# Other constants in the estimate that resumes background work in a hybrid decoder layer (one core of Trainium2)

## The chip, the core and the metric

The program runs on one core of one Trainium2 chip. A core has a matrix engine (TensorE, PE in the profile), a vector engine (VectorE, DVE), a scalar engine (ScalarE, ACT), GpSimd (POOL) and a queue engine (SyncE, SP) from which most of the DMA transfers are issued. Each engine works through its own instructions in order. The metric is the device time of one execution in microseconds.

## The reference

One step of one decoder layer, for a new sequence of 512 tokens ("prompt") and for eight sequences that each get one new token ("sample"), with the same weights, in float32:

```python
mod = silu(c) @ w_ada + b_ada                      # 6 x 2048 modulation values per sequence
h = modulate(rmsnorm(x, g_norm_mix), sh1, sc1)
proj = h @ w_in                                    # 2048 -> 1536 + 3360 columns
att = banded_attention(q, k, v, sinks)             # 16 heads, window 128, ALiBi
rw, S, last_row = rwkv7_mix(p_rwkv, ...)           # 16 heads, S_t = S diag(w) + (S a) b^T + v k^T
x = x + gt1 * (concat(att, rw) @ w_out)
h2 = modulate(rmsnorm(x, g_norm_ffn), sh2, sc2)
gate, up = split(h2 @ w_ffn_in)
x = x + gt2 * ((silu(gate) * up) @ w_ffn_out)      # 5632 hidden
y = rmsnorm(x, g_norm_final)
```

The outputs are y, the last keys and values, the RWKV states and the last projection rows, for prompt and sample.

## The kernel before

**Main work.** All 520 columns (512 prompt tokens and 8 sample tokens) are kept as two halves of 260. Each weight tile of 128 output columns is worked off in slices of 128 rows of the contraction. `unit` loads four slices of weights (256 KB), copies them to a rounded high part (`wh`, on ACT) and the remainder (`wl`, on DVE), and `mm3` issues six matmuls of 260 columns for one slice: high weights with the high and the low part of the activations, low weights with the high part, each for two halves. This text calls these six a *slice* of main work. `main_tile` runs 16 slices for a tile of `w_in` or `w_ffn_in`; `part_tile`, `wout_part` and `wout_half` do the same for pieces of `w_in` during the start-up and for `w_out`.

**Background work.** Everything else before the FFN is written as Python generators that run while the program is built: the modulation weights (`h_part` with `ada_part` in the start-up, `ada_gen` for the other four sixths), the preparation of RWKV for one pair of heads (`rwkv_prep1`, `rwkv_prep2`), the triangular solve and then the chain over 16 chunks of 32 tokens (`rwkv_rest`), the RWKV of the samples, the attention of prompt and sample, the loading of the concatenated result and half of the second norm. A generator issues some instructions, then yields.

**The estimate.** After each slice the kernel calls `pump`. It adds the assumed time of a slice to an estimated TensorE clock (`now`) and resumes, in the order of their start, each generator whose last instructions should be done by then (`job[1] <= now`). Background instructions go through `Paced` objects (`self.px`): each call of an engine adds an assumed duration, a base and a part per column, to that engine's estimated clock, not before the instruction before it in the same step is done (`spent`), and 0.1 for the way to the next engine. So a step's instructions are reckoned one after the other. For the modulation weights, whose matmuls don't go through `Paced`, the durations are written out. The estimate exists only while the program is built: it decides the order in which instructions are issued, and leaves no instruction in the program. A later pass of the compiler puts them in the order in which each engine runs them, and moves instructions that it thinks not ready behind others.

**The stages.** Up to about 151 us (start-up), the first modulation values and the first five tiles of `w_in` are made in five stages of 2, 2, 4, 4 and 4 slices per tile, with the modulation of the next stage behind each (`h_part`, and `drain` at its end). Then 22 tiles of `w_in` are made in the order that RWKV needs, with RWKV pairs, solve, chain and `ada_gen` behind them; 12 more tiles (`spills`, queries, keys and values) are put in where RWKV is late and otherwise at the end. One chain step (two per chunk) is two small matmuls with a tile position, a DVE and an ACT instruction that move the result to `Z`. One step of `ada_gen` is a DMA of 256 KB and four matmuls with a tile position; it yields twice after each. From about 925 us, `wout_part` runs with the attention behind it, and `wout_half` with half of the norm. The FFN, from about 1240 us, has its order written out and calls no `pump`.

Of the kernel before, what the change touches and what calls it, by code (L numbers as in the profile page):

```python
# [8 lines left out]
F32R = mybir.dt.float32r  # L9
# [22 lines left out]
class Paced:  # L32


    def __init__(self, kern, eng, per, base):
        self.kern, self.eng, self.per, self.base = kern, eng, per, base

    def __getattr__(self, name):
        f = getattr(self.eng, name)

        def call(out, *a, **kw):
            if name == "dma_start":
                self.kern.spent(self.eng, 1.0, 1.5)
            else:
                per = self.per
                if name == "matmul" and a[0].dtype == F32R:
                    per /= 4
                self.kern.spent(self.eng, self.base + per * math.prod(out.shape[1:]), 0.1)
            return f(out, *a, **kw)  # L49
        return call  # L50


class PacedCore:
    def __init__(self, kern):
        nc = kern.nc
        self.nc = nc
        self.tensor = Paced(kern, nc.tensor, 0.0017, 0.06)
        self.vector = Paced(kern, nc.vector, 0.0011, 0.08)
        self.scalar = Paced(kern, nc.scalar, 0.001, 0.2)
        self.gpsimd = Paced(kern, nc.gpsimd, 0.0023, 0.1)  # L60
        self.sync = Paced(kern, nc.sync, 0, 0)


class Kern:
    def __init__(self, tc, I, O, upto="all"):
        self.tc, self.nc, self.I, self.O, self.upto = tc, tc.nc, I, O, upto
        self.n = 0
        self.bg = []
        self.free, self.done_at = {}, 0.0
        self.px = PacedCore(self)  # L70
        self.nada = 0
        self.sample_done = self.kv_done = self.decode_done = False
        self.cat_out, self.cat_in = set(), 0
        self.psc = None
        self.squares = [None, None]
# [44 lines left out]
        self.free[self.nc.tensor] = self.free.get(self.nc.tensor, 0.0) + us  # L120
        return self.free[self.nc.tensor]

    def pump(self, us=0.62):

        self.now(us)
        for job in list(self.bg):
            if job[1] > self.now():
                continue
            self.done_at = self.now()
            if next(job[0], "end") == "end":  # L130
                self.bg.remove(job)
            job[1] = self.done_at

    def start(self, gen):
        self.bg.append([gen, 0.0])
# [136 lines left out]
    def ada_part(self, f):  # L272

        nc = self.nc
        ps = self.aux_c(f // 2 % 2)
        for kg in range(4):
            tag, n = (("RR", 2), ("L3", 3), ("As", 1), ("L3", 3), ("RR", 2), ("L3", 3))[self.nada % 6]
            self.nada += 1
            raw = self.rc.tile([P, 1024], F32, tag=tag, bufs=n, name=self.nm("araw"))
            nc.sync.dma_start(raw, self.I["w_ada1"][f // 2, kg])  # L280
            self.ada_mm(ps, raw, kg, 0, 256)
            self.spent(nc.tensor, 0.45)
            self.done_at += 0.7
            yield
        yield from self.ada_finish(f, 2, ps)
# [9 lines left out]
    def ada_gen(self):  # L295
        nc = self.px
        for c in (GT1, SH2, SC2, GT2):
            for q in range(4):
                ci = c // 4 + q
                ps = self.hold("ada")  # L300
                for k in range(KD):
                    raw = self.w.tile([P, 512], F32, tag="ar", bufs=3, name=self.nm("ar"))
                    nc.sync.dma_start(raw, self.I["w_ada2"][ci - 8, k])
                    for j in range(4):
                        self.nc.tensor.matmul(
                            ps[32 * j:32 * j + 32, 0:128], self.cT[:, k, :], raw[:, j * 128:(j + 1) * 128],
                            start=k == 0, stop=k == KD - 1, tile_position=(0, 32 * j), skip_group_check=True,
                        )
                    self.spent(self.nc.tensor, 0.3)
                    yield  # L310
                    yield
                res = self.w.tile([P, 512], F32, tag="ar", bufs=3, name=self.nm("adar"))[:, 0:128]
                nc.scalar.copy(res, ps[:, 0:128])
                yield
                p2 = self.aux("adT")
                nc.tensor.transpose(p2[:, 0:128], res, self.ident)
                nc.vector.tensor_tensor(
                    self.mod[:, 4 * ci:4 * ci + 4, :], p2[:, 0:128].rearrange("p (f t) -> p f t", f=4)[:, :, 0:9],
                    self.par[:, P_BA + 4 * ci:P_BA + 4 * ci + 4].unsqueeze(2).broadcast_to([P, 4, 9]), ALU.add)
# [963 lines left out]
    def wout_half(self, h, kept):  # L1283

        while self.cat_in < KD:
            self.pump()
        for o in range(0, KD, 2):
            mt = lambda: self.ps_m.tile([P, 2, 512], F32, tag="m", name=self.nm("po"))
            ps = mt()
            for j in range(2):  # L1290
                if o + j not in kept:
                    pool = dict(pool=self.wk, bufs=6) if o in (2, 6, 10) else {}
                    u = self.unit(self.I["w_out"][o + j, :, 12 * 128:16 * 128], **pool)
                    if pool:
                        kept[o + j] = u
                wh, wl = kept.get(o + j, u)
                for kk in range(4):
                    s = slice(kk * 128, (kk + 1) * 128)
                    self.mm3(ps, P, wh[:, s], wl[:, s], *self.cat[1], kk, kk == 0, kk == 3, ((h, j),))
                    self.pump(0.4)  # L1300
                if o == KD - 2:
                    self.accumulate_half(o + j, 1, ps[:, j:j + 1], GT1, h)
                    ps = mt()
            if o < KD - 2:
                self.accumulate_half(o, 2, ps, GT1, h)
# [233 lines left out]
```

## Time and profile before

| | us |
|---|---|
| median of 3 runs | 2763.02 |
| lowest, highest | 2754.31, 2765.76 |
| the profiled execution | 2761.62 |
| its span, first to last instruction | 2759.8 |

The rows of the profile used here have these forms. A row of the order of time gives start, duration (us), engine, line, operation, what is written from what, shapes, and how many instructions are merged; a bracket gives the idle time ahead and what ended it. A float32 matmul that isn't in the rounded format has two records each, so `psc<-Z,L x4` is one chain step of two matmuls (the first step of a chunk; `psc<-Z,LS` is the second), and `ada<-ar,cT x8` is one ada group of four. `pm` are main matmuls. A row by stretch gives the stretch and its length, then the busy time of PE, of the weight loads (PEld), DVE, ACT and POOL with their instructions, the granted TensorE clock (1.00 is full speed), the share of the DMA engines' time, and GB/s. A row of waits gives the waiting engine, tile and line, what it waited for, the total, how often, and the longest. Durations of matmuls overlap, so distances are taken from start to start. A few matmul records can be missing.

### The profile page before, as it was taken

Reading aid. Unit: us, or ns where it says so; the run is one execution under the profiler, and the core shown is the slowest. Engines: PE = TensorE matmul, PEld = TensorE weight load, DVE = VectorE, ACT = ScalarE, POOL = GpSimd, SP = SyncE. Lnnn points to the kernel's source line nnn. Section 1 sums busy time; section 2 is a strip of 40 time slices with the busy share of each in tenths; the row PEclk is TensorE's granted clock in tenths of the full one; section 3 lists DMA queues with packets and bytes.
Section 4 is the critical chain, followed back from the end, with each engine's and each line's share of the span. In section 5 each row is a group of like instructions: output and inputs, shape, how many; then the busy total and the mean of one; then the engine's idle time right before and its main releaser. Section 6 shows DMA issues by size and latency. Waiting matters only on the chain.

```text
span 2759.8 us, 58911 instructions
## 1 busy us (share of the span) xinstructions
PE 2679.3 (97%) x24461; PEld 2479.0 (90%) x24461; DVE 1356.5 (49%) x3266; ACT 923.4 (33%) x1816; POOL 223.6 (8%) x300
## 2 busy tenths in 40 slices
PE   7899999999999999989999999999999999999998
PEld 5577777887787898979999999999999999999997
DVE  2465677767755465682434343434343434343436
ACT  3133445455432344552222222222222222222225
POOL 1012122222111000130000000000000000000004
PEclk9899999999989999999999999999999999999999
DMA  8865554555556732322222222222222222222223
GB/s 296 308 200 149 153 152 141 161 150 151 175 163 206 255 133 100 113 80 92 91 93 90 93 92 93 92 92 93 92 93 92 92 93 92 93 92 93 90 96 110
DMA packets 189900, 354.25 MB, mean 128 GB/s; under 512 B 27665, under 2 KB 38849, under 8 KB 189345
## 3 DMA queue, kind: packets, MB, share of 16 engines
q1 hardware_dynamic: 185584, 339.30, 37.1%
q0 software_dynamic: 3408, 10.15, 1.2%
q8 instruction: 191, 3.13, 0.5%
q10 hardware_dynamic: 640, 1.05, 0.1%
q14 instruction: 77, 0.62, 0.1%
HBM read 332.86 MB, written 18.55 MB: 127 GB/s over the span
## 4 chain that ended last, share of the span: by engine, by line
PE 59%; DVE 2%; DMA 1%; ACT 1%; POOL 0%; issue 0%; DVEq 0%; SPq 0%; ACTq 0%; POOLq 0%
PE pm L98 36%; PE pf L98 18%; PE po L98 3%; PE pl L49 1%; PE pO L49 0%; PE pt L49 0%; PE psc L49 0%; DVE wl L91 0%; DVE x L1178 0%; DMA raw<-in_w_fi 0%; DVE h2L L49 0%; DVE u L49 0%; ACT h2H L49 0%; DMA raw<-in_w_out 0%; POOL u L49 0%
## 5 line engine op out<-in xcount | busy, mean ns | idle before, releaser
L88 ACT CAST wh<-raw 128x512 fp32r<-128x512 f32 (+2 forms) x751 | 460.9, 615 | 1266.8 <-PE pm L98 807.1
L91 DVE TENSOR_TENSOR wl<-raw,wh 128x512 fp32r<-128x512 f32 (+2 forms) x751 | 522.3, 697 | 690.2 <-ACT wh L88 688.8
L98 PE MATMUL pm<-h2H,wh 128*128 128x260 f32 x2816 | 571.2, 282 | 2.2 <-ACT wh L88 1.2
L98 PE MATMUL pm<-h2L,wh 128*128 128x260 f32 x2816 | 572.1, 283 | 0.7 <-DVE h2L L49 0.4
L98 PE MATMUL pm<-h2H,wl 128*128 128x260 f32 x2816 | 572.4, 283 | 0.0
L98 PEld LDWEIGHTS pm<-h2H,wh 128*128 128x128 f32 x2816 | 435.9, 188 | 2.9 <-ACT wh L88 1.3
L98 PEld LDWEIGHTS pm<-h2L,wh 128*128 128x128 f32 x2816 | 435.0, 188 | 1.7 <-DVE h2L L49 1.5
L98 PEld LDWEIGHTS pm<-h2H,wl 128*128 128x128 f32 x2816 | 436.3, 188 | 0.0
L98 PE MATMUL pm<-hH,wh 128*128 128x260 f32 (+1 forms) x1248 | 297.6, 318 | 2.8 <-ACT hH L143 1.6
L98 PE MATMUL pf<-gH,wh 128*128 128x260 f32 x1312 | 266.8, 283 | 0.0
L98 PE MATMUL pf<-gH,wl 128*128 128x260 f32 x1312 | 266.4, 282 | 0.0
L98 PE MATMUL pf<-gL,wh 128*128 128x260 f32 x1312 | 266.4, 282 | 0.0
L98 PE MATMUL pm<-hL,wh 128*128 128x260 f32 (+1 forms) x1248 | 264.7, 292 | 0.2 <-DVE hL L144 0.2
L98 PE MATMUL pm<-hH,wl 128*128 128x260 f32 (+1 forms) x1248 | 262.5, 291 | 0.0
L98 PEld LDWEIGHTS pm<-hH,wh 128*128 128x128 f32 (+1 forms) x1248 | 195.9, 192 | 51.8 <-issue 33.1
L1167 DVE SCALAR_TENSOR_TENSOR x<-pf,mod,x 128x512 f32<-128x512 f32 x160 | 120.1, 750 | 215.1 <-PE pf L98 215.1
L98 PEld LDWEIGHTS pf<-gH,wl 128*128 128x128 f32 x1312 | 203.4, 188 | 0.0
L98 PEld LDWEIGHTS pf<-gL,wh 128*128 128x128 f32 x1312 | 203.2, 188 | 0.0
L98 PEld LDWEIGHTS pf<-gH,wh 128*128 128x128 f32 x1312 | 203.2, 188 | 0.0
L98 PEld LDWEIGHTS pm<-hH,wl 128*128 128x128 f32 (+1 forms) x1248 | 197.6, 192 | 6.0 <-issue 1.8
L98 PEld LDWEIGHTS pm<-hL,wh 128*128 128x128 f32 (+1 forms) x1248 | 198.0, 192 | 5.4 <-issue 2.0
L1186 POOL TENSOR_TENSOR acc<-sqh 128x260 f32<-128x260 f32 x4 | 3.0, 742 | 1662.1 <-ACT sqh L1183 1471.3
(372 smaller groups left out, 3100.2 us busy)
## 6 DMA issues: line engine op xcount, KB each, us to landing
raw<-in_w_fi SPq DMA_DIRECT2D x352, 256.0 KB, 2.5
ar<-in_w_ada SPq DMA_DIRECT2D x256, 256.0 KB, 3.1
raw<-in_w_fo SPq DMA_DIRECT2D x176, 256.0 KB, 2.5
raw<-in_w_in SPq DMA_DIRECT2D x148, 256.0 KB, 3.6
araw<-in_w_ada SPq DMA_DIRECT2D x64, 512.0 KB, 6.0
raw<-in_w_out SPq DMA_DIRECT2D x74, 256.0 KB, 2.9
catl<-catd SPq DMA_DIRECT2D x16, 256.0 KB, 2.8
x<-in_x SPq DMA_DIRECT2D x4, 780.0 KB, 7.8
```

What stands on the lines that cost most here:

```text
L49: return f(out, *a, **kw)
L88: nc.scalar.copy(wh[:, :n], raw[:, :n])
L91: nc.vector.tensor_tensor(wl[:, :n], raw[:, :n], wh[:, :n].bitcast(F32), ALU.subtract)
L98: nc.tensor.matmul(ps[:m, bank, :HB], w, a[:, k, h, :], start=first and i == 0, stop=last and i == 2, skip_group_check=True,)
L1167: nc.vector.scalar_tensor_tensor(x[:, :, 0:256], ps[:, :, 0:256], self.mod[:, gt + o, 0:1], x[:, :, 0:256], ALU.mult, ALU.add)
L1186: nc.gpsimd.tensor_tensor(acc, sq[:, 0], sq[:, 1], ALU.add)
```

## The change

It touches only the estimate:

- A slice of main work counts 0.73 instead of 0.62 (`pump`), in `wout_half` 0.37 instead of 0.4.
- On TensorE, a matmul with a tile position counts 0.05, whatever its size, and a transpose 0.12. Other matmuls count 0.03 and 0.002 per column instead of 0.06 and 0.0017; in the rounded format, a quarter of the whole instead of a quarter of the part per column.
- A group of modulation matmuls counts 0.3 instead of 0.45 in the start-up, 0.15 instead of 0.3 afterwards.
- Any TensorE instruction of the background sets `switched`, and a `pump` in which it was set ends with 0.2 more on the clock, once for all generators resumed in it.

```diff
-                per = self.per
-                if name == "matmul" and a[0].dtype == F32R:
-                    per /= 4
-                self.kern.spent(self.eng, self.base + per * math.prod(out.shape[1:]), 0.1)
+                us = self.base + self.per * math.prod(out.shape[1:])
+                if name == "transpose":
+                    us = 0.12
+                elif name == "matmul":
+                    us = 0.05 if kw.get("tile_position") else us / 4 if a[0].dtype == F32R else us
+                if self.eng is self.kern.nc.tensor:
+                    self.kern.switched = True
+                self.kern.spent(self.eng, us, 0.1)
...
-        self.tensor = Paced(kern, nc.tensor, 0.0017, 0.06)
+        self.tensor = Paced(kern, nc.tensor, 0.002, 0.03)
...
-    def pump(self, us=0.62):
+    def pump(self, us=0.73):
...
             job[1] = self.done_at
+        if self.switched:
+            self.switched = False
+            self.now(0.2)
...
-            self.spent(nc.tensor, 0.45)
+            self.spent(nc.tensor, 0.3)
+            self.switched = True
             self.done_at += 0.7
...
-                    self.spent(self.nc.tensor, 0.3)
+                    self.spent(self.nc.tensor, 0.15)
+                    self.switched = True
                     yield
                     yield
...
-                    self.pump(0.4)
+                    self.pump(0.37)
```

More of the change, by code (lines that the diff above doesn't have):

```diff
@@ L68, in __init__ @@
         self.bg = []
-        self.free, self.done_at = {}, 0.0
+        self.free, self.done_at, self.switched = {}, 0.0, False
         self.px = PacedCore(self)
```

## The prediction

> **What bounds the kernel now.** I read the page first (span, busy engines), then the busy time by stage, then the order of time on TensorE (PE), then the waits.
>
> ```profile
> span 2759.8 us, 58911 instructions
> PE 2679.3 (97%) x24461; PEld 2479.0 (90%) x24461; DVE 1356.5 (49%) x3266; ACT 923.4 (33%) x1816; POOL 223.6 (8%) x300
> ```
>
> ```profile
> 42.00:151.00 109.00, 96.12 (x856) 67.59 (x856) 50.32 (x143) 24.30 (x58) 10.33 (x13) 0.87 0.83 302
> 151.00:925.00 774.00, 752.80 (x8402) 613.73 (x8403) 517.31 (x1352) 337.14 (x720) 147.12 (x196) 0.97 0.55 164
> 925.00:1160.00 235.00, 232.29 (x2051) 213.17 (x2050) 130.09 (x431) 101.11 (x266) 5.77 (x10) 0.98 0.42 142
> 1160.00:1240.00 80.00, 67.72 (x490) 63.66 (x490) 68.14 (x152) 46.30 (x89) 29.68 (x35) 0.96 0.28 98
> 1240.00:2760.00 1520.00, 1505.79 (x12526) 1504.67 (x12524) 583.07 (x1171) 399.55 (x661) 28.86 (x31) 1.00 0.27 93
> ```
>
> The columns after the stretch are its length, the busy us of PE, weight load, DVE, ACT and POOL, the granted clock, the DMA share and GB/s. PE is the bound in every stage. The last 1520 us are the FFN, which calls no pump: nothing that the change sets reaches them. Its room is the first 1240 us, and there above all the 774 us from 151 to 925, where the projections of mixers A and B are the main work and the RWKV chain and the modulation weights (ada) run behind them. PE is busy for 752.8 of these 774 us, so little can be won from waits. What an estimate can move there is **how often PE changes between main and small matmuls**, and what one change costs stands in the order of time:
>
> ```profile
> 400.71 0.41 PE L98 MATMUL pm<-hH,wh 128*128 128x260 f32 x2
> 401.17 0.31 PE L49 MATMUL psc<-Z,L 128*32 128x64 f32 x4
> 401.40 0.51 PE L98 MATMUL pm<-hL,wh 128*128 128x260 f32 x2
> 401.75 0.39 PE L98 MATMUL pm<-hH,wl 128*128 128x260 f32 x2
> 402.08 0.43 PE L305 MATMUL ada<-ar,cT 128*32 128x128 f32 x8
> 402.43 0.50 PE L98 MATMUL pm<-hH,wh 128*128 128x260 f32 x2
> 402.86 0.34 PE L49 MATMUL psc<-Z,LS 128*64 128x64 f32 x4
> 403.13 0.51 PE L98 MATMUL pm<-hL,wh 128*128 128x260 f32 x2
> 403.48 0.40 PE L98 MATMUL pm<-hH,wl 128*128 128x260 f32 x2
> ...
> 404.52 0.42 PE L305 MATMUL ada<-ar,cT 128*32 128x128 f32 x8
> 404.78 0.28 PE L49 MATMUL psc<-Z,L 128*32 128x64 f32 x4
> 404.99 0.51 PE L98 MATMUL pm<-hH,wh 128*128 128x260 f32 x2
> 405.33 0.40 PE L98 MATMUL pm<-hL,wh 128*128 128x260 f32 x2
> 405.57 0.40 PE L98 MATMUL pm<-hH,wl 128*128 128x260 f32 x2
> ...
> 406.61 0.43 PE L305 MATMUL ada<-ar,cT 128*32 128x128 f32 x8
> 406.97 0.34 PE L49 MATMUL psc<-Z,LS 128*64 128x64 f32 x4
> 407.23 0.51 PE L98 MATMUL pm<-hH,wh 128*128 128x260 f32 x2
> 407.58 0.40 PE L98 MATMUL pm<-hL,wh 128*128 128x260 f32 x2
> ```
>
> Two main matmuls follow two others after 0.24 us (405.33 to 405.57), so a slice of six takes 0.72 us. A burst of small matmuls takes, from its own start to the start of the second main pair behind it, its price plus one pair (0.24) less the gap ahead of it (0.09: from 401.75 a pair should end at 401.99, the ada group starts at 402.08); so I subtract 0.15. An ada group alone: 0.35 to the main pair at 402.43, plus the 0.34 that a first pair takes (404.99 to 405.33), less 0.15: **0.54 us**. A chain step alone: 0.43 (401.17 to 401.75) or 0.47 (402.86 to 403.48). An ada group with a chain step right behind it: 0.66 (404.52 to 405.33) or 0.82 (406.61 to 407.58). So a chain step that shares its burst saves 0.54 + 0.43 - 0.66 = 0.31 or 0.54 + 0.47 - 0.82 = 0.19, **0.25 us on the mean**.
>
> There are 256 chain steps (8 pairs of heads, 16 chunks, two steps each). Going through the order of time from 160 to 960 us, 124 of them stand in a burst without ada, the first and the last here, and 132 share one:
>
> ```profile
> 270.96 0.31 PE L49 MATMUL psc<-Z,L 128*32 128x64 f32 x4
> ...
> 891.88 0.30 PE L49 MATMUL psc<-Z,L 128*32 128x64 f32 x4
> ```
>
> **The change part by part.** It adds, removes and re-sizes no instruction; it moves when generators are resumed. The numbers of this paragraph are the estimate's own, worked out from the constants, not times of the chip. Main slices go from 0.62 to 0.73. An ada group comes at every second pump, before and after, because its generator yields twice and its end is never late (its two steps add 2.5 + 0.3 before, 2.5 + 0.15 + 0.2 after). A chain step issues two matmuls of 64 columns, a DVE copy and an ACT copy. After its matmuls it is done later by 0.1 + (0.08 + 0.0011 x 64 + 0.1) + (0.2 + 0.001 x 64 + 0.1) + 0.2 = 0.914. Before, the next pump is 0.62 on: not due, and it waits for the pump after, where ada is resumed first and pushes the clock on by 2.8. That is the steady pattern at 404.52 and 406.61: one step in every two slices, behind ada. After, the next pump is 0.2 (the burst) + 0.73 = 0.93 on: **due, by 0.016**. So every chain step comes at the very next slice, half of them at pumps that have no ada. The triangular solve of the next pair (31 steps on DVE) has 0.74 left in the same reckoning and goes to every slice as well.
>
> What a chain step really takes is in the two copies behind it:
>
> ```profile
> 401.95 0.23 DVE L49 COPY Z<-psc 32x64 f32<-32x64 f32 x1
> 402.39 0.20 ACT L49 COPY Z<-psc 32x64 f32<-32x64 f32 x1
> 405.18 0.23 DVE L49 COPY Z<-psc 32x64 f32<-32x64 f32 x1 [1.26 <-PE psc L49]
> 405.45 0.20 ACT L49 COPY Z<-psc 32x64 f32<-32x64 f32 x1 [1.19 <-DVE Z L49]
> ```
>
> Undisturbed 0.87 us (404.78 to 405.65), behind other DVE work 1.42 (401.17 to 402.59). From a chain step to the end of the next slice are 0.21 + 0.34 + 0.24 + 0.24 = 1.03 us. The stretch at 401 to 403 shows what happens when steps come at every slice: the program does not wait, it lets main matmuls go ahead, and the step drops into the middle of a slice, alone. The one at 401.17 stands after one pair of its slice, the one at 402.86 one pair *past* the ada group that it was meant to share. I therefore expect nearly all steps to lose their company: the 128 that fall to slices without ada surely, and most of the other 128. I take 45 that still share, against 132: 87 x 0.25 = **+22 us**. Bounds: 110 left sharing (+5) and 10 (+30).
>
> Waits grow with the steps that follow closely:
>
> ```profile
> PE psc L49 <- ACT Z L49: 6.3, 14, 1.2
> PE pu L49 <- DVE L L49: 4.8, 1, 4.8
> ```
>
> The 6.3 us before chain steps belong to the half that stands alone; twice as many such steps give **+5** (0 to +10). Short waits also seem to cost clock. The 20 us with the wait of 1.15 us in the first row have a granted clock of 0.91:
>
> ```profile
> 304.60 0.34 PE L49 MATMUL psc<-Z,LS 128*64 128x64 f32 x4 [1.15 <-ACT Z L49]
> ```
>
> ```profile
> 300.00:320.00 20.00, 18.24 (x182) 15.21 (x179) 16.96 (x42) 6.76 (x17) 1.82 (x3) 0.91 0.45 132
> ```
>
> That is a loss of 20 x 0.09 = 1.8 us; I take one more such stretch, **+2** (0 to +6). [...]
>
> Against this stand the jumps that the estimate makes too large now. Thirty-two small matmuls in one step (pG, pA, pY) count 0.214 to 0.269 apiece now, with the 0.1 between them, and 0.15 after, so other jobs are resumed less far ahead of their data. The single wait of 4.8 us comes in such a stretch; I take **-3** of it (-5 to 0).
>
> **The start-up** (42 to 151 us) has its own clock: a modulation slice (512 KB by DMA, four matmuls) is followed by 0.7 in the estimate, so two pumps of 0.62 before; after, 0.2 + 0.73 = 0.93 covers it, one pump.
>
> ```profile
> 103.06 0.64 PE L267 MATMUL psc<-araw,cT 128*32 128x256 f32 x8
> 105.27 0.64 PE L267 MATMUL psc<-araw,cT 128*32 128x256 f32 x8
> ```
>
> ```profile
> 80.00:100.00 20.00, 18.96 (x136) 12.31 (x129) 7.39 (x21) 4.65 (x10) 1.81 (x1) 0.66 0.98 372
> 100.00:120.00 20.00, 17.02 (x178) 11.92 (x176) 9.55 (x34) 2.64 (x6) 0.00 (x0) 1.00 0.68 230
> ```
>
> While main work runs, a modulation slice is used every 2.2 us, and the DMA engines move 230 GB/s; in the 20 us before they reach 372. The whole stretch moves 302 GB/s x 109 us = 32.9 MB, 88.5 us at 372 GB/s, so even use of the slices could win at most 20 us. But each of its four stages ends in a tail that no transfer shortens (modulation, norm, split, first matmul), and PE takes its slices in order. I take less than a third, **-6** (-13 to +3).
>
> Attention and the output projection (925 to 1240): the same PE bursts, whose meeting is left to chance; the norm's steps are counted in pumps, not in time. 0, with 4 us either way. The transposes (0.278 to 0.12) and the pump of 0.37 belong here.
>
> **Sum.** +22 + 5 + 2 - 3 - 6 = +20 us. The profiled execution took 2761.62 us, 1.8 more than its span and 1.4 less than the median of 2763.02. Forecast: 2761.6 + 20 = 2781.6, about **2782 us**, 0.7% slower.
>
> **The rivals.**
>
> *The steps keep their company.* A step that is late by more than the way to the next ada group joins it, and the margin of 0.016 is thin: one more charge on the DVE clock (a weight unit charges it 0.61) and the step waits for the ada pump as now. For it: undisturbed steps need 0.87 us and would be ready. Against it: where steps follow at every slice now, they stand alone. With 110 left sharing: +5, waits +2, -3, -6: 2760, no change.
>
> *The start-up decides.* If company is kept and the start-up wins two thirds of its 20 us, 2761.6 - 13 - 3 = 2746: faster. It decides from the point where the DMA share of the stretch from 42 to 151 (0.83 in its row) passes 0.93. Against it: PE would have to take a slice per 1.3 us in order without waiting.
>
> *The clock falls in the dense stretch.* With chain, solve and ada at every slice, PE does more tiny matmuls in a row. What that can do:
>
> ```profile
> 760.00:780.00 20.00, 20.00 (x139) 17.76 (x138) 5.22 (x17) 4.92 (x12) 0.93 (x1) 0.74 0.42 125
> ```
>
> PE is busy throughout, yet the clock is 0.74, a loss of 5.2 us in 20. Four more such windows: 2782 + 21 = 2803. [...] Against it: the clock is 1.00 in most of the stage, which is full of bursts already.
>
> **How the numbers follow.** Forecast 0.46, its own range 2771 to 2795 (its two largest terms moved towards their ends); company kept 0.30; start-up 0.14; clock 0.10. The range takes in the forecast's range, the first rival and about half of the two others: 2747 to 2800. A measurement of this kernel tells about 0.5% (13.8 us) from no change. Slower by more: 0.38 out of the forecast's 0.46 (its low end is within) and the clock's 0.10: 0.48. Faster by more: most of the start-up rival, 0.12. Within: 0.40.
>
> **What would show it.** Right: chain steps (psc from Z) about one slice apart, bursts without ada rising from 124 to some 200. The last projection tiles come at the same slice, but the chain's last step earlier than 892 us. Start-up: modulation slices 1.3 to 1.7 us apart instead of 2.2, and the stretch some 6 us shorter. Wrong: steps still two slices apart, or 110 and more beside ada; then the sum loses its largest term. If the time moves after 1240 us, the whole reading is wrong.

## The result, and the profile after

The changed kernel takes 2798.28 us (median of 4 runs, 2794.42 to 2800.08); the kernel before took 2758.66 us in the runs beside it (4 runs, 2752.75 to 2765.76). The ratio is **1.0137, 95% interval 1.0107 to 1.0168**: slower by 1.4%, where the forecast was 0.7%. The profiled execution took 2798.36 us, 36.7 more than the one before.

The head of the page of the changed kernel:

```profile
span 2796.3 us, 58933 instructions
PE 2706.7 (97%) x24461; PEld 2479.2 (89%) x24461; DVE 1346.1 (48%) x3266; ACT 924.9 (33%) x1816; POOL 216.4 (8%) x300
```

PE has as many matmuls as before (x24461) and the other engines are as busy as they were: no work was added. To see where the 36.7 us lie, the span is cut at the first ada group, the first matmul of the output projection (`po`) and the first FFN matmul. Rows by stretch of the kernel before, then of the changed one (length; busy us of PE, PEld, DVE, ACT, POOL; granted clock; DMA share; GB/s):

```profile
42.00:154.00 112.00, 99.07 (x866) 69.69 (x866) 53.02 (x151) 26.46 (x62) 10.33 (x13) 0.87 0.82 299
154.00:933.30 779.30, 758.16 (x8463) 619.56 (x8463) 518.67 (x1352) 338.79 (x723) 147.12 (x196) 0.98 0.55 165
933.30:1216.10 282.80, 269.38 (x2301) 247.86 (x2299) 174.47 (x536) 129.16 (x319) 31.36 (x40) 0.97 0.38 131
1216.10:2759.00 1542.90, 1528.11 (x12690) 1525.71 (x12690) 602.76 (x1210) 413.98 (x692) 32.94 (x35) 1.00 0.27 93
```

```profile
42.00:160.20 118.20, 103.27 (x868) 65.48 (x868) 53.44 (x149) 25.30 (x62) 9.93 (x13) 0.91 0.81 283
160.20:967.70 807.50, 780.66 (x8463) 622.54 (x8463) 508.96 (x1355) 340.49 (x724) 140.69 (x196) 0.98 0.54 160
967.70:1252.50 284.80, 270.07 (x2301) 249.36 (x2301) 172.64 (x533) 129.07 (x317) 30.83 (x40) 0.97 0.37 128
1252.50:2796.00 1543.50, 1528.10 (x12690) 1525.64 (x12690) 603.26 (x1210) 414.68 (x692) 33.13 (x35) 1.00 0.27 93
```

**Start-up +6.2 us, RWKV stage +28.2, attention and output projection +2.0, FFN unchanged** (1543.7 and 1543.8 us to the ends of the spans). In the RWKV stage PE is *busy* 22.5 us longer with the same 8463 matmuls, at the same clock of 0.98. Matmuls that take longer at the same number and clock point to changes between kinds of matmul. The order of time of the changed kernel shows them:

```profile
420.39 0.28 PE L102 MATMUL pm<-hH,wl 128*128 128x260 f32 x1
420.60 0.30 PE L53 MATMUL psc<-Z,L 128*32 128x64 f32 x4
420.83 0.39 PE L102 MATMUL pm<-hH,wl 128*128 128x260 f32 x1
421.06 0.28 PE L102 MATMUL pm<-hH,wh 128*128 128x260 f32 x1
421.27 0.43 PE L313 MATMUL ada<-ar,cT 128*32 128x128 f32 x8
421.63 0.39 PE L102 MATMUL pm<-hH,wh 128*128 128x260 f32 x1
421.86 0.40 PE L102 MATMUL pm<-hL,wh 128*128 128x260 f32 x2
422.19 0.34 PE L53 MATMUL psc<-Z,LS 128*64 128x64 f32 x4
...
846.36 0.34 PE L53 MATMUL psc<-Z,LS 128*64 128x64 f32 x4
```

Chain step, ada group and chain step come within 1.6 us, each alone, even inside a pair of main matmuls (`x1`). This is what the prediction expected of every slice. The chain now ends at 846.36 us, where its last step stood at about 899 before (the 891.88 us in the prediction is the last step that stands without ada, not the last of all).

Counting groups of small matmuls between main ones through the order of time (**bursts**), the RWKV stage has 465 where it had 402. Of the 256 chain steps 85 share a burst with ada, where 133 did (the prediction counted 132). In the start-up there are 51 bursts where there were 29.

The view of waits, for PE in the RWKV stage, adds up to 24.9 us; the same view of the kernel before adds up to 19.8. Its first rows, and then the row for ada from the kernel before (total us, times, longest):

```profile
PE ada L313 <- DMA ar<-in_w_ada: 9.8, 11, 3.3
PE psc L53 <- ACT Z L53: 5.9, 18, 0.8
PE pu L53 <- DVE L L53: 3.6, 1, 3.6
PE pm L102 <- DVE wl L95: 1.9, 2, 1.1
```

```profile
PE ada L305 <- DMA ar<-in_w_ada: 3.6, 3, 1.5
```

The 5.1 us more are in the wait of ada for its weights (3.6 to 9.8), not in front of chain steps (6.3 to 5.9).

In the start-up the changed kernel uses the modulation slices closer to each other, as predicted, but each in a burst of its own:

```profile
100.38 0.64 PE L274 MATMUL psc<-araw,cT 128*32 128x256 f32 x8
100.95 0.51 PE L102 MATMUL pm<-hH,wh 128*128 128x260 f32 x2
101.30 0.41 PE L102 MATMUL pm<-hL,wh 128*128 128x260 f32 x2
101.55 0.40 PE L102 MATMUL pm<-hH,wl 128*128 128x260 f32 x2
101.88 0.64 PE L274 MATMUL psc<-araw,cT 128*32 128x256 f32 x8
```

The slices are 1.5 us apart instead of 2.2, with one slice of main work between them; the drains at the stages' ends, where several slices used to stand together (5, 12, 7 and 7 in one burst before, a single burst of 8 now), have less left to do. The DMA share of the stretch stayed at 0.81 to 0.82: the slices did not arrive sooner on the whole. PE waits less for modulation slices up to the first ada group (4.0 us, 5.8 before), but its main matmuls wait more for the copies of their own weights (6.1 us, 1.2 before).

### The profile page after: what moved, and what is told of

It is laid out like the page before. It is cut to its first block, busy times and chain, and to the rows that moved or that the text cites. A ratio compares the mean times of both kernels' runs of the same rounds, so it can differ in the third digit from the quotient of the medians.

```text
span 2796.3 us, 58933 instructions
## 1 busy us (share of the span) xinstructions
PE 2706.7 (97%) x24461; PEld 2479.2 (89%) x24461; DVE 1346.1 (48%) x3266; ACT 924.9 (33%) x1816; POOL 216.4 (8%) x300
## 4 chain that ended last, share of the span: by engine, by line
PE 85%; DVE 5%; DMA 5%; ACT 2%; issue 1%; POOL 1%; SPq 0%; DVEq 0%; ACTq 0%; POOLq 0%
PE pm L102 50%; PE pf L102 18%; PE po L102 5%; PE psc L53 3%; PE ada L313 3%; DMA ar<-in_w_ada 1%; DVE wl L95 1%; PE psc L274 1%; PE pA L53 1%; PE pl L53 1%; DMA raw<-in_w_out 1%; ACT wh L92 1%; DMA araw<-in_w_ada 1%; PE ssq L386 1%; PE pt L53 1%
## 5 line engine op out<-in xcount | busy, mean ns | idle before, releaser
L102 PE MATMUL pm<-hH,wl 128*128 128x260 f32 (+1 forms) x1248 | 275.4, 295 | 6.0 <-DVE wl L95 5.9
```

The source lines that it names most:

```text
L102: nc.tensor.matmul(ps[:m, bank, :HB], w, a[:, k, h, :], start=first and i == 0, stop=last and i == 2, skip_group_check=True,)
```

## The experiments

The theory: what costs is the number of bursts, because two sums in the estimate slipped below the new distance of 0.93 to the next pump: a chain step's 0.914 and the 0.7 of a start-up slice. The rivals: the other constants themselves, waits, and the clock. "The built order" in the expectations is the order in which the instructions stand in the program of each engine.

**e1, chain back to two slices.** The changed kernel with

```diff
-            self.done_at += 0.2
+            self.done_at += 0.23
```

behind both chain steps.

> The changed kernel, with 0.23 instead of 0.2 added after each of the two chain steps in the estimate (0.944 left instead of 0.914, so not covered by 0.2 + 0.73 = 0.93): chain steps fall back to every second slice. In the built order 120 of 256 chain steps then share a burst with ada (85 in the changed kernel, 133 before) and the RWKV stage has 423 bursts of small matmuls (465 changed, 402 before). Theory (the loss is the number of bursts, because the chain became due at every slice): from the first ada group to the first matmul of the output projection 807 us fall to 785 to 792, the start-up stays at 160, the whole is 2776 to 2784. Rival (the other constants, or longer waits for DMA and weights, make the loss): the stage stays above 800 and the whole above 2790. Rival (clock): the stage shortens only where the clock rises, by 0.01 or more over the stage.

**e2, start-up slices back to two pumps.** The changed kernel with

```diff
             self.switched = True
-            self.done_at += 0.7
+            self.done_at += 1.0
```

> The changed kernel, with 1.0 instead of 0.7 added after a group of modulation matmuls in the start-up: not covered by 0.93, so one modulation slice at every second pump, as before. In the built order the start-up has 29 bursts instead of 51, and all counts behind it are those of the changed kernel. Theory (the start-up lost by the same cause as the chain: slices used singly at every pump make more bursts): first ada group at 154 instead of 160 us, everything behind it as in the changed kernel, the whole 2790 to 2794. Rival (the start-up lost 6 us to something else, DMA order or the other constants): first ada group stays at 159 to 161.

**e3, both edits.**

> The changed kernel with both edits, 0.23 after chain steps and 1.0 after modulation groups in the start-up: two thresholds put back, all new constants kept. Theory (the two thresholds are the whole loss, and they add): both gains together, 2769 to 2778, within 0.6% of the kernel before. Rival (the new sizes of pump, small products and transposes cost time of their own): 2785 or more.

**e4, the chain at every slice in the kernel before.**

```diff
-            self.done_at += 0.2
+            self.done_at -= 0.1
```

> The kernel before, with its old constants, and 0.1 taken off instead of 0.2 added after each chain step (0.614 left, covered by the old pump of 0.62): chain steps at every slice and nothing else changed. In the built order 77 chain steps share a burst with ada and the RWKV stage has 460 bursts. Theory: the RWKV stage takes 779 + 22 to 28 us, the start-up stays at 154, the whole is 2780 to 2790. Rival (the small products' and the switch's constants as such cost the time): within 5 us of the kernel before.

Rows by stretch of the stage up to the first ada group in e2, and of the RWKV stage in e1, e3 and e4:

```profile
42.00:153.20 111.20, 97.67 (x875) 67.76 (x874) 54.10 (x155) 26.84 (x62) 10.33 (x13) 0.88 0.84 304
```

```profile
160.40:959.50 799.10, 771.17 (x8463) 624.82 (x8463) 515.84 (x1354) 336.98 (x722) 138.47 (x196) 0.97 0.55 161
```

```profile
154.30:948.90 794.60, 766.35 (x8463) 621.13 (x8463) 516.37 (x1354) 337.11 (x722) 138.44 (x196) 0.97 0.56 162
```

```profile
154.60:968.90 814.30, 787.04 (x8463) 624.99 (x8463) 516.77 (x1354) 339.12 (x724) 142.46 (x196) 0.97 0.54 158
```

e2 (2794.4 us) settles the start-up: with 29 bursts again the first ada group comes at 153.2 us instead of 160.2, while the stage behind it keeps its 465 bursts and its 805.4 us. e4 shows that the old constants lose as much as the new ones once the chain comes at every slice: 35.0 us in the RWKV stage, above the 22 to 28 expected, and 2799.1 in all (2780 to 2790 expected). But e1 (2790.7 us) and e3 (2784.5) regain only 8 and 13 of the stage's 28 us, not the 15 to 22 expected of e1, both come out close to what their rivals named (2790, 2785), and e3 still takes 1.0074 of the time before (interval 1.0045 to 1.0104). The two thresholds are not the whole loss: with them put back there are still 423 bursts, not 402, and 25.6 and 26.2 us of waits. So the constants that bear on this stage were tried alone.

**e5, e6, e7: one new constant each in the kernel before.** e5 has the slice at 0.73; e6 the new durations of small products, transposes and ada groups; e7 only `switched` with its 0.2.

> The kernel before with one of the four new constants: a slice counts 0.73. A chain step (0.914 left) is still due at the second pump; a start-up slice (0.7) is covered by one. In the built order 126 of 256 chain steps share a burst with ada (133 before), the RWKV stage has 414 bursts (402 before, 465 changed), the start-up 51 (29 before, 51 changed). Theory (a burst more costs about half a us, which is what the three runs with other thresholds gave once the time lost to the granted clock is taken off: 29.6 us for 63 bursts, 32.6 for 58, 14 for 21): start-up +6, RWKV stage +6, the whole about 2774. Rival (a larger pump resumes work further ahead of its data and so costs waits, whatever the bursts): RWKV stage +12 or more and PE idle there above 24 us.

> The kernel before with the new durations of small products, transposes and ada groups alone; the pump stays 0.62 and nothing is added for a burst. In the built order 123.5 chain steps share a burst, 415 bursts in the RWKV stage, 29 in the start-up. Theory: start-up 0, RWKV stage +6.5, the whole about 2768 to 2770. The prediction took a gain of 3 us from smaller jumps of the estimate; if that is real and bursts are not the price, 2757 to 2761. Rival (these durations are what the two repaired thresholds left over): RWKV stage +14.

> The kernel before with the 0.2 per burst alone: the next pump is 0.82 on. A chain step (0.914) is still due at the second pump, a start-up slice (0.7) at the first. In the built order 113 chain steps share a burst, 425 bursts in the RWKV stage, 51 in the start-up. Theory: start-up +6, RWKV stage +11, the whole 2776 to 2782. Rival (only the two thresholds matter, and the chain's is not crossed here): start-up +6, RWKV stage within 4 us, the whole 2764 to 2770.

e5 (2783.7 us) and e7 (2790.7) lose more than expected (RWKV stage +14.2 and +19.6 us). In e5 the rival's two conditions hold: 12 us or more, and waits of 26.2 us. So a larger slice costs some 6 us of waits beside its bursts. The waits that grow are those of chain steps for ACT (6.3 us before) and of ada for its weights (3.6):

```profile
PE psc L49 <- ACT Z L49: 13.6, 28, 1.8
PE ada L305 <- DMA ar<-in_w_ada: 5.6, 8, 2.1
```

e6 takes 2773.9 us (ratio 1.0039, 1.0023 to 1.0054), with an RWKV stage 2.1 us *shorter* than before, 8.6 below what its bursts promised, and a stage of attention and output projection 9.5 us longer:

```profile
154.50:931.70 777.20, 754.65 (x8463) 613.82 (x8463) 526.34 (x1354) 331.99 (x719) 138.14 (x196) 0.99 0.56 166
931.70:1224.00 292.30, 275.12 (x2301) 253.43 (x2299) 173.94 (x534) 127.26 (x317) 31.27 (x40) 0.94 0.37 124
```

The clock differs here, 0.99 in the one stage and 0.94 in the other. To compare kernels, the time lost to the clock is therefore taken off: the sum, over stretches of 10 us, of length times one minus the granted clock. In e6 it is 11.4 us in the RWKV stage, where it was 19.3; without waits and clock that stage is 5 us longer than before, not shorter, and its 13 bursts more agree with that.

**e8 to e11: fewer bursts.** e8 is the kernel before, with all background work resumed at every second pump from the first chain step to the output projection:

```diff
+        self.npump += 1
...
-            if job[1] > self.now():
+            if job[1] > self.now() or self.alt and self.npump % 2 and not job[2]:
                 continue
+            self.anywhere = False
...
-            job[1] = self.done_at
+            job[1], job[2] = self.done_at, self.anywhere
...
+            self.anywhere = s < 30
...
+            self.anywhere = c % 2 == 1 and c < 15
```

The last two lines free the solve and, in every second chunk, what follows the chain's second step (the next chunk's first step may then come at any pump). `alt` is set at the first chain step and cleared at the output projection; while it is set, ada yields once instead of twice. In e9 `pump` counts 0.73 and the start-up slice 1.0 as well; e10 is e9 with `c % 4 == 1`; e11 is e3 with the lines of e8.

> The other direction: the kernel before with its old constants, but from the first chain step to the output projection background work is resumed at every second pump only, all jobs together (the triangular solve, on DVE alone, and a chain's first step of every second chunk also at the others), and ada at each of these. In the built order 167 chain steps share a burst with ada, the RWKV stage has 357 bursts (402 before); the chain ends with some 8 steps behind the last projection slice. Theory (the price is the burst): 45 bursts at half a us are -22 us, the uncovered steps at about 1 us +8, together 2740 to 2755, faster than before. Rival (the price is not the number of bursts but waits and clock): 2757 or more.

> The kernel that resumes all work at every second pump, with a slice at 0.73 (and 1.0 in the start-up, so that its slices stay two pumps apart). The generators then run further ahead, and the chain's last step falls 24 slices ahead of the end of the projections instead of behind them. In the built order 157 chain steps share a burst with ada, 370 bursts in the RWKV stage, 29 in the start-up. Theory (0.3 to 0.4 us for each burst, without waits and clock): 32 bursts fewer than before are -10 to -13; waits as in the other kernels with a changed slice +0 to +7; no uncovered tail: 2750 to 2762, at or below the kernel before, and over 20 us below the alternating kernel with the old slice. Rival (alternating itself costs what it saves, by later steps or a lower clock): 2766 or more.

> The same, with a chain's first step allowed at the other pumps in every fourth chunk instead of every second. 169 chain steps share a burst, 358 bursts in the RWKV stage, and the chain ends 16 slices ahead of the end, some 18 us, about what the norm and the copy behind it take. Theory: 44 bursts fewer are -13 to -18; waits +0 to +7; the tail 0 to +4: 2746 to 2762. Rival (the tail decides): slower than the kernel with every second chunk.

> All new constants of the changed kernel with the two thresholds put back, and work resumed at every second pump as in the two others. 156 chain steps share a burst, 375 bursts in the RWKV stage, 29 in the start-up. Theory (what the estimate's constants are matters only through the bursts and the tail): 27 bursts fewer than before are -8 to -11, waits +0 to +7, so 2753 to 2764; 48 fewer than with the thresholds put back alone (2784.5), so 15 to 25 us below that. Rival (the new constants cost time of their own, by running ahead of data): within 10 us of 2784.5.

e8 has its 357 bursts and is slower than before all the same (2785.3 us, ratio 1.0078, 1.0052 to 1.0104). The order of time at the end of its projections shows why:

```profile
928.75 0.40 PE L99 MATMUL pm<-hH,wl 128*128 128x260 f32 x2
...
937.45 0.48 PE L49 MATMUL psc<-Z,LS 128*64 128x64 f32 x4
...
942.84 1.09 PE L49 MATMUL pt<-cst,RR 128*128 128x128 f32 x4 [4.55 <-DVE RR L49]
...
954.34 0.99 PE L99 MATMUL po<-cH,wh 128*128 128x260 f32 x3 [6.37 <-ACT cH L146]
```

Behind the last main matmul PE works off the rest of the chain, waits for the norm and then for the split of the result: 25.6 us without cover, not the 8 expected. Up to there the stage took 776.2 us, 3 less than before, though it lost 26.6 us to the clock instead of 19.3.

e9 ends the chain in time and gains 9.4 us in the RWKV stage. That is near the expected 10 to 13, but not for the expected reason: 2.7 us of it are shorter waits and 4.0 a higher clock, so that only 2.7 are left for 32 bursts fewer. The whole comes to 2761.4 us, **ratio 1.0000 (0.9990 to 1.0011)**: the next stage gives it back.

```profile
152.60:922.50 769.90, 750.32 (x8463) 617.16 (x8462) 518.09 (x1350) 334.81 (x717) 142.00 (x198) 0.98 0.56 165
922.50:1215.00 292.50, 274.76 (x2299) 253.38 (x2300) 178.61 (x539) 130.66 (x322) 30.24 (x38) 0.95 0.40 129
```

Waits of PE in this second stretch, and the row that answers to it in the kernel before:

```profile
PE po L99 <- ACT cH L146: 6.3, 3, 3.0
```

```profile
PE po L98 <- ACT cH L143: 0.4, 1, 0.4
```

The chain's last step stands at 899 us in both, but the projections end at 921 instead of 933: the way from the chain through norm, store, load and split to the output projection is now the one that ends last. Of the 6.3 us, 1.5 lie ahead of the stretch, so this wait is some 4.4 of its 9.7 us more; 15.5 us lost to the clock instead of 8.5, partly during the same waits, go with the rest; how the two divide it stays open. e10 has 12 bursts fewer than e9 and is slower (1.0061, interval 1.0042 to 1.0080): its chain ends at 915 us and the output projection starts 11.0 us behind the last projection, where 0 to 4 were expected. The rival named for it was right. e11 takes 2774.6 us (1.0045, 1.0029 to 1.0061), 10 below e3 where 15 to 25 were expected, so that its rival's condition (within 10 us of e3) is just met: the RWKV stage is 11.7 us shorter than in e3, and the next stage 9.6 longer. No version beats the kernel before.

**e12, ada moved away from its company.** e9, with ada's groups at the odd pumps, and nothing else:

```diff
+                    self.anywhere = self.alt
                     yield
                     if not self.alt:
                         yield
+                    while self.alt and self.npump % 2 == 0:
+                        self.anywhere = True
+                        yield
```

> The alternating kernel with a slice at 0.73 and the chain's free steps in every second chunk, with one thing moved: ada groups are issued at the odd pumps, where no other work comes, instead of the even ones. The chain keeps its slices (first step at slice 150, last at 600, as there). In the built order 63 chain steps share a burst with ada (157 there) and the RWKV stage has 480 bursts (370 there). Over the twelve kernels profiled so far the length of the RWKV stage goes with its bursts at 0.31 us each. Theory (a burst costs 0.31 us, whichever constant splits it): 110 more are +34 us over that kernel's 770 us, so a stage of 800 to 808 and a whole of 2790 to 2800. Prediction's own price (0.25 for each of 94 chain steps that lose company): +24, a whole of 2785. Rival (what costs is that work is resumed ahead of its data, and bursts only go along with it): the chain's steps are no nearer to each other than there, so within 10 us of 2761.

```profile
154.50:966.20 811.70, 787.02 (x8463) 631.65 (x8462) 509.44 (x1349) 335.40 (x717) 145.05 (x201) 0.97 0.54 157
```

```profile
422.21 0.43 PE L308 MATMUL ada<-ar,cT 128*32 128x128 f32 x8
422.57 0.51 PE L99 MATMUL pm<-hH,wh 128*128 128x260 f32 x2
...
424.21 0.34 PE L49 MATMUL psc<-Z,LS 128*64 128x64 f32 x4
424.47 0.42 PE L308 MATMUL ada<-ar,cT 128*32 128x128 f32 x8
424.83 0.51 PE L99 MATMUL pm<-hH,wh 128*128 128x260 f32 x2
```

The stage grows by 41.8 us against e9 (expected 30 to 38) for 110 bursts more, with 19.8 us of waits against 17.1 and 12 us more lost to the clock; without these two, 27 us, 0.24 per burst. The profiled execution is the slowest of e12's four. The whole is 2796.2 us (ratio 1.0103, 1.0060 to 1.0145), in the 2790 to 2800 of the theory and above the 2785 of the prediction's own price. Work is resumed no further ahead of its data here than in e9, so the rival that bursts only go along with early resumption falls.

All kernels, by their profiled executions (us; the start-up is the time of the first ada group; joined are chain steps in a burst with ada):

| kernel | joined | bursts | start-up | RWKV stage | its waits | lost to the clock | attention, w_out |
|---|---|---|---|---|---|---|---|
| before | 133 | 402 | 154.0 | 779.3 | 19.8 | 19.3 | 282.8 |
| changed | 85 | 465 | 160.2 | 807.5 | 24.9 | 18.7 | 284.8 |
| e1 | 120 | 423 | 160.4 | 799.1 | 25.6 | 25.2 | 288.0 |
| e2 | 85 | 465 | 153.2 | 805.4 | 24.8 | 15.0 | 287.7 |
| e3 | 120 | 423 | 154.3 | 794.6 | 26.2 | 20.2 | 285.1 |
| e4 | 77 | 460 | 154.6 | 814.3 | 25.3 | 21.7 | 284.0 |
| e5 | 126 | 414 | 162.0 | 793.5 | 26.2 | 22.2 | 283.4 |
| e6 | 124 | 415 | 154.5 | 777.2 | 20.7 | 11.4 | 292.3 |
| e7 | 113 | 425 | 164.1 | 798.9 | 26.5 | 20.0 | 286.1 |
| e8 | 167 | 357 | 152.5 | 801.8 | 33.5 | 35.6 | 288.0 |
| e9 | 157 | 370 | 152.6 | 769.9 | 17.1 | 15.3 | 292.5 |
| e10 | 169 | 358 | 154.1 | 785.8 | 30.8 | 22.5 | 291.9 |
| e11 | 156 | 375 | 153.8 | 782.9 | 22.4 | 24.5 | 294.7 |
| e12 | 63 | 480 | 154.5 | 811.7 | 19.8 | 27.8 | 289.7 |

Read the bursts against the stage. Without e8, whose stage ends in its uncovered tail, a straight line through the other thirteen rises by **0.31 us per burst** and misses the stages by a standard deviation of 7.5 us. With waits and clock taken off it rises by 0.30 (standard error 0.02) and misses by 3.1. This is an average, not one price: the nine kernels without alternation alone give 0.41 (standard error 0.03), while e9, e10 and e11, compared with the kernel before in the same way, save only 0.08 to 0.18 for each burst that they have fewer. Why joining saves less than splitting costs stays open.

What one split costs also stands in the rows. The prediction's subtraction, repeated over all bursts of one ada group, one chain step or both in the kernel before (at full clock, without waits), gives medians of 0.55 us for ada alone, 0.43 and 0.46 for the two kinds of chain step alone, and 0.66 and 0.82 for ada with each. So company saves 0.32 or 0.20 us, 0.26 on the mean. The lone bursts of the changed kernel have the same medians.

In the start-up, the ten kernels with 29 bursts have their first ada group at 152.5 to 154.6 us, the four with 51 at 160.2 to 164.1: between the two means 7.8 us for 22 bursts, 0.36 each, the longer waits for weight copies included.

An ada group and a chain step differ from a main matmul in two things, the form of the weights (128*32 or 128*64 against 128*128) and the number format, and the rows tell the two apart. In the kernel before, a chain step of the same form as ada (128*32) starts 0.26 us behind the start of the ada group (404.52 to 404.78 in the prediction), a step of another form (128*64) 0.36 (406.61 to 406.97), though all three are plain float32; a main matmul, in the rounded format, starts 0.36 behind as well. These are also the medians over 53, 50 and 99 such places. So a change of form goes with about 0.10 us here, whatever the format.

## Why the prediction was right in its sign, and where it was wrong

**What bounds the kernel, and what a split costs: right.** The forecast was 2782 us, the result 2798, within the range of 2747 to 2800 by 2 us and above the forecast's own 2771 to 2795. The price of 0.25 us for a chain step that loses its company, taken from one stretch of 7 us, stands beside 0.26 from all such bursts of the kernel before and 0.31 per burst from thirteen kernels. The FFN kept its time.

**The RWKV stage: right in sum, +26 predicted, +28.2 measured, in part by luck.** Its terms: for lost company +22 predicted, by 87 chain steps; 48 lost it. But other products were split off as well (bursts without ada or a chain step rose from 24 to 41), so the bursts rose by 63. At 0.30 that is 18.9 us, at the 0.41 of the nine kernels 25.9. So the near hit of this term is luck: too many steps were counted, and the other products were left out. Waits +5, less 3 for smaller jumps, predicted; +5.1 measured. But neither place was right: the time in front of chain steps hardly changed (6.3 to 5.9), ada waited 6.2 us longer for its weights, and the single wait of 4.8 us only fell to 3.6. Clock +2 predicted, -0.6 measured. Bursts, waits and clock together give 23.4 or 30.4 us; the measured 28.2 lies between.

**The start-up: wrong, and this step carries the error.** "Even use of the slices could win at most 20 us" and "I take less than a third, -6" counted what the DMA could win and left out what PE would pay. The same edit makes 22 bursts more, and at the prediction's own 0.25 that is +5.5. Measured: +6.2, and -7.0 when the bursts go (e2). The DMA gain did not come, at a share of 0.81 (0.82 before): the 1.8 us that PE waits less for modulation slices are more than taken back by the 4.9 us that it waits longer for the copies of the main weights, which the prediction did not count either. 12.2 of the 16.8 us between forecast and profiled execution lie here, 2.2 in the RWKV stage, 2 in attention and output projection, whose 0 ± 4 held.

**The rivals.** Company was not kept: 85, below the 110 of that rival. The start-up had the other sign. The rival of the falling clock gave 2803, the number nearest to the result, for a wrong reason: with 63 bursts more the stage has 0.98 in both rows, and the loss went from 19.3 to 18.7.

**The threshold of 0.016: the mechanism was right, but not alone.** Putting it back regains 8.4 (e1) or 12.9 (e3) of the 28.2 us in the RWKV stage; the two differ by what the clock costs. The rest came from constants that cross no threshold of the steady chain: each of the three alone leaves 12 to 23 bursts more than before.

## What to carry to other kernels

Where small matmuls run between main ones, count the bursts in the built order before weighing anything else: here each that is split off costs 0.25 to 0.4 us, whichever estimate does it, and their number is known before a run. Do not expect the same back for each that is joined: here it was 0.08 to 0.18. Price an edit with it in every stage that it reaches, also where another resource seems to set the pace. And when background work is packed more tightly, look at what it feeds next: a saving is kept only while its last step stays far enough ahead of the stage that needs it (here more than 21 us).

## What the runs showed of the hardware

The granted clock fell while PE had work all the time, to 0.56 in this row of e12:

```profile
800.00:820.00 20.00, 20.00 (x111) 16.88 (x111) 7.07 (x37) 4.20 (x10) 1.15 (x2) 0.56 0.33 100
```

PE is busy for all 20 us. What stands just ahead of it is this:

```profile
795.96 0.68 PE L49 MATMUL pLx<-sX,slw 128*128 128x8 f32 x4
...
797.71 0.80 PE L99 MATMUL pm<-hL,wh 128*128 128x260 f32 x2
```

Since 793.48 us, up to 796.57, PE works off products of 8 and 16 columns for the samples (`pLx`); then a pair of main matmuls takes 0.80 us instead of 0.40. The kernel before, the changed one and e9 to e12 each have a fall of the clock that begins between 760 and 800 us, during such products or within 3 us behind them; in stretches of 10 us from the first ada group on, the lowest there are 0.61, 0.83, 0.83, 0.50, 0.67 and 0.50. Another fall follows a wait: at 862 us in the changed kernel, just behind ada's wait of 3.3 us, to 0.50 in the 2 us up to 864. No run changes `pLx`, so it isn't shown that these products are the cause.

The time lost to the clock in the RWKV stage lies between 11 and 28 us, e8 with its tail left out, without following bursts (19.3 us at 402, 15.0 and 18.7 at 465) or the sum of waits (22.4 us of waits and 24.5 of clock in e11, 24.8 and 15.0 in e2). It moves the stage by as much as 16 bursts do: e1 and e3, which have the same counts there, differ by 4.5 us in the stage and by 5.0 in what the clock costs.
